# Routing ahead of a mixture of experts: places of two row blocks at once, the last block's expert input on VectorE, gathered rows unfilled, and the fixed experts' first products ahead of the one-hots

## The chip, the cores and the metric

The kernel runs on one core of a Trainium2 chip. The metric is device time in microseconds of one execution; the figure of a kernel is the median of several. The profile is of one execution, whose time is given beside its span.

## The reference

One layer of a hybrid diffusion backbone over 1024 latent tokens of width 1024: a token mixer (a bidirectional state-space branch and a pooling branch, merged by gates), a projection and a first layer norm, then a hierarchical mixture of experts and a second layer norm. The change touches the seam between the mixer and the experts, so this is the part to see:

```python
lg = hf @ w_rg + b_rg                       # 4 groups; the best one is taken
le = (hf @ w_re + b_re)[best group]         # 8 experts in it
top_v, top_i = lax.top_k(le, 2)
w = p_grp * softmax(top_v)
...                                         # every token goes to 2 of 32 experts
y[e] = (silu(x_e @ w_eg[e]) * (x_e @ w_eu[e])) @ w_ed[e]     # 1024 -> 512 -> 1024
out = sum over the two experts of w * y
```

All is f32. Each expert has 6 MiB of weights.

## The kernel before

The kernel is written with a tile framework that orders the instructions of each engine by itself: it models when each could start and lets those that come earlier in the program go first. `tc.issue_after(x)` queues an instruction behind x on its own engine, `tc.high_priority` lets one go ahead of its place in the text. Each engine, SyncE's and POOL's queues too, then runs in the order so fixed.

**The output projection and the choice (loop of lines 1137 to 1179).** The 1024 tokens are 8 row blocks of 128. For block t, `wout` multiplies by the output matrix and adds the residual in r; `turn` transposes r; eight matmuls give 36 router logits (line 1158); `stats` gives mean and 1/deviation (ag, rs); the logits come out on line 1164 (lgt). `choose(t)` (lines 989 to 1023) is a chain of some 17 small VectorE instructions: best group, best expert, second expert, as one-hots o12 and their sum A (line 1020), and running counts bsum. Then r is normalized on ScalarE (line 1166), the expert input hx = r G2 + B2 is made (lines 1172, 1173) and written to h2_d by POOL's queue (line 1174), and r, scaled by the first norm's weights (lines 1177, 1178), goes to r0_d (line 1179). For blocks 0 to 6 hx is made on VectorE and r on POOL; for block 7 the other way round.

**The places.** `place(t)` (lines 1025 to 1051) counts with two matmuls how many tokens ahead of each one chose the same expert, keeps what falls to the three fixed experts (29 to 31, 32 rows each), and adds with a one-hot product to `pidf`, a column of row numbers of the fixed experts' 96 rows. Places are taken with a lag of five blocks: 0, 1, 2 at blocks 5, 6, 7, and 3 to 7 after block 7. The other 29 experts get row blocks by rank of their counts: lines 1267 to 1305 work out rank and capacity on 32 partitions, lines 1306 to 1319 spread that to the tokens, lines 1328 to 1338 form one-hots (ohl, ohh) of all 2048 choices and 16 products that give `pid`, the row numbers of 50 row blocks, and lines 1250 to 1259 turn these into gather and scatter indices xidx and yidx. `tab` (line 1349) holds the experts by rank; SyncE reads it to know which weights to load.

**The experts.** `block` gathers 128 rows of h2_d by index (line 1239, an indirect DMA on POOL's queue), transposes them (line 1389), multiplies by gate and up weights, and by the down weights, scales and scatters. Indices out of range are skipped by the gather, so the first use of each of four buffers xe is preceded by a fill with zeros on POOL (line 1237). The first block is that of the three fixed experts: exact f32 products (line 1406), 32 rows of each, 16 steps for gate and up and 8 for down, in each step two passes over the three experts. Then the dynamic experts follow in the order "DEQEESPESPSPSPSPSPSS" of capacities 256 (D, two blocks), 192 (E), 128 (S), 64 in pairs (P) and 32 in fours (Q), and at the end a loop over experts that overflow.

**Weights.** `load_w` fills slots of one megabyte, 16 in all (`NSA` + `NSB`), in turn. The fixed experts take 24 tiles of 768 KB (three transfers each), so tiles 16 to 23 go into slots 0 to 7 once the first products have read these. Tiles 14 and 15 are issued by POOL behind the first gather (lines 1263 to 1265). All other weights go through SyncE's queue in program order (line 1222).

**PSUM.** `st` and `tr` have one bank each, `mm` four, `py` two. `pos` (counts of all tokens) holds `tr` until line 1316, the ranks hold `st` until line 1312, and `block` transposes through `st` and `tr`.

Of the kernel before, what the change touches and what calls it, by code (L numbers as in the profile page):

```python
# [11 lines left out]
F32 = mybir.dt.float32  # L12
# [8 lines left out]
P = 128  # L21
# [82 lines left out]
LAG = 5  # L104
# [37 lines left out]
def _emit(tc, nc, es, ins, out, dbg, stop):  # L142
# [810 lines left out]
    gp = rg.enter_context(pool("gp", side="right"))  # L953
    r0g = row(gp, ins["ln"][0], "r0g")
    r0b = row(gp, ins["ln"][1], "r0b")
    lgt = gp.tile([P, NT, 36], F32, name="lgt")
    G2 = row(gp, mod_d[0, 2 * D:3 * D], "G2")
    B2 = row(gp, mod_d[0, D:2 * D], "B2")
# [21 lines left out]
    ohhf = gp.tile([P, NT, 2, 4], F32R, name="ohhf")  # L980
# [8 lines left out]
    def choose(t):  # L989
# [28 lines left out]
        A = gp.tile([P, NE], F32, name="A", bufs=LAG + 1)  # L1018
# [5 lines left out]

    def place(t, A):
        def tl(shape, name):
            return gp.tile([P] + shape, F32, name=name, bufs=2)

        T.matmul(pos[:, t], cst[:, C_SPRE], A, start=True, stop=False)
        T.matmul(pos[:, t], ones, bsum[:, t], start=False, stop=True)  # L1030


        pf = pos[:, t, NE - NF:]
        okf = tl([NF], "okf")
        V.tensor_scalar(okf, pf, float(FIX_CAP), None, op0=OP.is_lt)
        pb = tl([NF], "pb")
        V.tensor_tensor(pb, pf, ct[:, 341:341 + NF], op=OP.add)
        of = tl([2, NF], "of")
        V.tensor_tensor(of, o12[:, :, t, NE - NF:], b1_(okf, 2), op=OP.mult)
        lp = tl([2, 2, NF], "lp")  # L1040
        V.tensor_tensor(lp[:, 0], of, b1_(pb, 2), op=OP.mult)
        V.tensor_tensor(lp[:, 1], of, b2(aid.rearrange("p (k t) -> p k t", k=2)[:, :, t], NF), op=OP.mult)
        lv = tl([2, 2], "lv")
        V.tensor_reduce(lv, lp, axis=AX.X, op=OP.add)
        lo = lv[:, 0]
        V.tensor_copy(ohhf[:, t, :, 0], lv[:, 1])
        ohlf = gp.tile([P, 2, P], F32R, name="ohlf", bufs=1)
        last = V.tensor_tensor(ohlf, b1_(iop, 2), b2(lo, P), op=OP.is_equal)
        for k in range(2):
            T.matmul(pidf, ohlf[:, k], ohhf[:, t, k], start=(t + k == 0), stop=(t == NT - 1 and k == 1))  # L1050
        return last

    def weights():
        S.activation(ge, ge, AF.Exp)
        pg = kept.tile([P, NT], F32, name="pg")
        V.tensor_reduce(pg, ge, axis=AX.X, op=OP.add)
        V.reciprocal(pg, pg)
        V.tensor_sub(v12[:, 1], v12[:, 1], v12[:, 0])
# [4 lines left out]
        V.tensor_tensor(wk[:, 1], wk[:, 0], v12[:, 1], op=OP.mult)  # L1063

    with pool("o_sb") as op_:
# [10 lines left out]
        bT2 = gp.tile([P, 4, P], F32, name="bT2")  # L1076
# [60 lines left out]
        for t in range(NT):  # L1137
# [106 lines left out]


    with pool("gq", side="right") as gq:
# [3 lines left out]
        def rows_of(pid, n, name, x, y=None):  # L1250

            fi = tl([n], name + "f")
            V.tensor_scalar(fi, pid, 0.0, 8192.0, op0=OP.is_equal, op1=OP.mult)
            V.tensor_tensor(fi, fi, pid, op=OP.add)
            gi = tl([n], name + "g")
            V.tensor_scalar(gi, fi, float(L + 1), -float(L), op0=OP.is_ge, op1=OP.mult)
            V.scalar_tensor_tensor(x, gi, -1.0, fi, op0=OP.add, op1=OP.add)
            if y is not None:
                V.tensor_scalar(y, fi, -1.0, None, op0=OP.add)

        rows_of(pidf[:, 0:1], 1, "fx", xfix)
        gathered.append(gather(xfix))
# [4 lines left out]
        e32 = slice(0, NE)  # L1267
        fixed, ecol = ct[e32, 337:338], ct[e32, 340:341]
        pc = bank("st")
        cr = pc[:, 0:NE]  # L1270
        cc = pc[e32, NE:NE + 1]
        T.matmul(cr, ones, bsum[:, NT], start=True, stop=True)
        T.matmul(cc, bsum[:, NT], ones[:, 0:1], start=True, stop=True)
        kr = tl([NE], "kr", NE)
        kc = tl([1], "kc", NE)
        V.scalar_tensor_tensor(kr, cr[e32], 32.0, ct[e32, 40:72], op0=OP.mult, op1=OP.add)
        V.scalar_tensor_tensor(kc, cc, 32.0, ct[e32, 336:337], op0=OP.mult, op1=OP.add)
        V.tensor_scalar(kr, kr, kc, None, op0=OP.is_gt)
        rk = tl([1], "rk", NE)
        V.tensor_reduce(rk, kr, axis=AX.X, op=OP.add)  # L1280
        V.scalar_tensor_tensor(rk, fixed, 64.0, rk, op0=OP.mult, op1=OP.add)

        ns_ = len(STEPS)
        cb2 = tl([2, ns_], "cb2", NE)
        V.tensor_scalar(cb2[:, 0], ct[e32, 144:144 + ns_], rk, None, op0=OP.is_gt)
        V.tensor_scalar(cb2[:, 1], ct[e32, 144:144 + ns_], rk, None, op0=OP.min)
        V.tensor_tensor(cb2, cb2, ct[e32, 152:152 + 2 * ns_].rearrange("p (a n) -> p a n", a=2), op=OP.mult)
        cols = tl([3], "cols", NE)
        V.tensor_reduce(cols[:, 0:2], cb2, axis=AX.X, op=OP.add)
        V.tensor_tensor(cols[:, 0:2], cols[:, 0:2], ct[e32, 338:340], op=OP.add)  # L1290
        cap = cols[:, 0:1]

        rem = tl([1], "rem", NE)
        V.tensor_tensor(rem, cc, cap, op=OP.subtract)
        nbx = tl([8], "nbx", NE)
        V.tensor_scalar(nbx, ct[e32, 72:80], rem, None, op0=OP.is_lt)
        nb = tl([1], "nb", NE)
        V.tensor_reduce(nb, nbx, axis=AX.X, op=OP.add)
        po = pc[e32, 64:65]
        T.matmul(po, cst[e32, C_SPRE, 0:NE], nb, start=True, stop=True)  # L1300
        ovs = tl([1], "ovs", NE)
        V.tensor_copy(ovs, po)
# [67 lines left out]

    scat = []

    def block(idx, w, ne, W=P):

# [264 lines left out]
```

## Time and profile before

| | |
|---|---|
| three runs | 2198.86, 2200.76, 2203.87 us; median 2200.76 |
| profiled execution | 2201.33 us, span 2199.5 us |
| busy share of the span | PE 92%, PE weight load 69%, VectorE 61%, ScalarE 41%, POOL 26% |
| mean granted TensorE clock | 0.968 of full speed |
| DMA moved | 441.90 MB, 201 GB/s over the span |

How to read it: busy shares are means over stages with different limits. The first row block's hx is made at 1453 us, the choice and the places run until about 1565, the routing until about 1585, the experts until about 2149, the second norm to the end. A time on the profile counts from the span's start. The granted clock is 1.0 at 2.4 GHz and 0.5 at 1.2 GHz.

### The profile page before, as it was taken

What the parts mean: (1) busy time and instruction counts of PE and PEld (TensorE: products, weight loads), DVE (VectorE), ACT (ScalarE), POOL (GpSimd) and SP (SyncE); (2) the same over time, 40 slices, a digit from 0 to 9 for tenths busy, and PEclk for the clock granted to TensorE, in tenths of its full rate; (3) what the DMA queues carried; (4) which work ended last, traced back from release to release, by engine and by line L of the source; (5) the groups of instructions that cost most, each with busy time, mean ns of one, the idle gap of its engine ahead of it and who ended that gap; (6) DMA issues with size and microseconds to landing.
All of it is one profiled execution on the core that took longest, in us unless ns stands there. A gap on an engine that the chain in (4) does not pass through costs nothing. (4 is left out here: it accounts for less than half of the span.)

```text
span 2199.5 us, 28490 instructions
## 1 busy us (share of the span) xinstructions
PE 2013.6 (92%) x10086; PEld 1524.3 (69%) x10086; DVE 1348.0 (61%) x1913; ACT 895.4 (41%) x1589; POOL 575.7 (26%) x547
## 2 busy tenths in 40 slices
PE   7998999999999999999989999989699899999984
PEld 4787788778777878788768877778455476554451
DVE  4644476677558676867646675587744485543376
ACT  4422254454444564545432232121143364543362
POOL 3243123233224333424200112243411021201003
PEclk8999999999999999999999999999699999999997
DMA  7132233333332333433367675535599999999965
GB/s 296 58 96 87 91 96 106 106 96 96 120 116 91 114 101 93 144 95 108 115 233 245 209 255 166 199 115 191 196 396 341 391 402 389 370 413 411 407 247 234
DMA packets 171899, 441.90 MB, mean 201 GB/s; under 512 B 19997, under 2 KB 54045, under 8 KB 160745
## 3 DMA queue, kind: packets, MB, share of 16 engines
q1 hardware_dynamic: 154282, 399.67, 51.5%
q0 software_dynamic: 9984, 26.75, 3.2%
q10 hardware_dynamic: 7488, 13.63, 1.7%
q8 instruction: 80, 1.31, 0.2%
q14 instruction: 65, 0.53, 0.1%
HBM read 403.01 MB, written 46.28 MB: 204 GB/s over the span
## 5 line engine op out<-in xcount | busy, mean ns | idle before, releaser
L186 PE MATMUL mm<-hh,whi 128*128 128x512 f32 x1024 | 414.8, 405 | 0.0
L188 PE MATMUL mm<-hh,wlo 128*128 128x512 f32 x1024 | 401.5, 392 | 4.2 <-DVE wlo L183 4.2
L187 PE MATMUL mm<-hl,whi 128*128 128x512 f32 x1024 | 400.8, 391 | 0.0
L188 PEld LDWEIGHTS mm<-hh,wlo 128*128 128x128 f32 x1024 | 192.9, 188 | 46.1 <-DVE wlo L183 4.6
L701 ACT ACTIVATE rb<-rb,tmx 128x128 f32<-128x128 f32 x512 | 163.0, 390 | 146.3 <-POOL rb L694 145.0
L186 PEld LDWEIGHTS mm<-hh,whi 128*128 128x128 f32 x1024 | 193.3, 189 | 38.4 <-issue 2.6
L187 PEld LDWEIGHTS mm<-hl,whi 128*128 128x128 f32 x1024 | 193.4, 189 | 35.7 <-issue 0.2
L1367 ACT ACTIVATE sh<-wb 128x512 fp32r<-128x512 f32 x280 | 169.7, 628 | 96.8 <-DMA wb<-in_w_e_dram 24.3
L1368 DVE TENSOR_TENSOR sl<-wb,sh 128x512 fp32r<-128x512 f32 x280 | 180.6, 686 | 39.1 <-ACT sh L1367 33.8
L183 DVE TENSOR_TENSOR wlo<-wraw,whi 128x1024 fp32r<-128x1024 f32 x65 | 82.7, 1272 | 186.1 <-ACT whi L182 186.0
L673 POOL TENSOR_TENSOR st<-st,gst 128x256 f32<-128x256 f32 x112 | 135.6, 1211 | 201.3 <-ACT st L658 120.0
L186 PE MATMUL mm<-zh,bhi 128*128 128x512 f32 x384 | 153.7, 400 | 8.5 <-ACT bhi L182 8.5
L188 PE MATMUL mm<-zh,blo 128*128 128x512 f32 x384 | 153.0, 398 | 1.1 <-DVE blo L183 1.1
L187 PE MATMUL mm<-zl,bhi 128*128 128x512 f32 x384 | 152.0, 396 | 0.3 <-DVE zl L183 0.3
L694 POOL TENSOR_SCALAR_AFFINE_SELECT rb<-rb 128x512 f32<-128x512 f32 x128 | 102.3, 805 | 173.0 <-DMA rb<-sr_d 168.7
L1239 POOL DMA_INDIRECT xe<-h_d,xidx x25 | 27.3, 1091 | 333.7 <-PE tr L1389 304.5
L1406 PE MATMUL mm<-wb,xh 128*64 128x512 f32 (+1 forms) x516 | 108.3, 599 | 0.3 <-ACT xh L1395 0.3
L182 ACT ACTIVATE bhi<-braw 128x1024 fp32r<-128x1024 f32 x48 | 50.8, 1059 | 140.5 <-PE mm L187 123.0
L518 DVE SCALAR_TENSOR_TENSOR xT<-craw,sm,xT 128x1284 f32<-128x1284 f32 x64 | 100.9, 1576 | 2.9 <-ACT xT L516 2.7
L182 ACT ACTIVATE whi<-wraw 128x1024 fp32r<-128x1024 f32 x65 | 68.3, 1050 | 76.5 <-PE mm L187 36.4
L187 PE MATMUL mm<-sl,xh 128*128 128x512 f32 x224 | 88.7, 396 | 5.2 <-DVE sl L1368 5.2
L186 PEld LDWEIGHTS mm<-zh,bhi 128*128 128x128 f32 x384 | 73.2, 191 | 26.0 <-ACT bhi L182 8.9
(471 smaller groups left out, 4094.0 us busy)
## 6 DMA issues: line engine op xcount, KB each, us to landing
wb<-in_w_e_dram SPq DMA_DIRECT2D x70, 1024.0 KB
wb<-in_w_e_dram SPq DMA_DIRECT2D x120, 512.0 KB
wb<-in_w_e_dram SPq DMA_DIRECT2D x142, 256.0 KB
wraw<-in_w_blk_dram SPq DMA_DIRECT2D x64, 512.0 KB
rb<-sr_d SPq DMA_DIRECT2D x128, 256.0 KB
F<-sr_d SPq DMA_DIRECT2D x64, 256.0 KB
wmr<-in_w_ada_dram SPq DMA_DIRECT2D x64, 256.0 KB
braw<-in_wa_blk_dram SPq DMA_DIRECT2D x32, 512.0 KB
```

Source lines behind the costliest of these rows:

```text
L182: S.activation(hi, src, AF.Copy)
L183: V.tensor_sub(lo, src, hi.bitcast(F32))
L186: T.matmul(ps, lh, rh, start=start, stop=False, **kw)
L187: T.matmul(ps, lh, rl, start=False, stop=False, **kw)
L188: return T.matmul(ps, ll, rh, start=False, stop=stop, **kw)
L518: V.scalar_tensor_tensor(o, raw[:, j:j + n], smc(SM_CW + b * KCONV + j), o, op0=OP.mult, op1=OP.add)
L673: G.tensor_tensor(nv, sv, gv[:, s, :, 2 * un:2 * un + 2].unsqueeze(3).to_broadcast([P, 2, 2, 64]), op=OP.mult)
L694: G.affine_select(rv, rv, pattern=[[0, 2], [0, 2], [sg, P]], base=0, channel_multiplier=-sg, compare_op=OP.is_ge, fill=NEG_BIG)
L701: S.activation(e, e, AF.Exp, bias=tmx[:, 0, 2 * n + ih, hd:hd + 1])
L1367: S.activation(hi, w, AF.Copy)
L1368: V.tensor_tensor(lo, w, hi.bitcast(F32), op=OP.subtract)
L1406: T.matmul(pss[0][i * W:(i + 1) * W], ls[0][0][:, k, i * W:(i + 1) * W], wt[:, i], start=(k == 0), stop=(k == nk - 1))
```

## The change

- `place(t0, t1)` takes the places of several blocks with one set of VectorE instructions, twice as wide for two. The schedule is `PLACE_AT`: blocks 0 and 1 at block 5, 2 and 3 at 6, 4 at 7, and after block 7 first 5 and 6, then 7.
- The last block's hx is made on VectorE, at high priority, in two instructions straight from r, mean and deviation, in place of POOL's two products of the normalized r.
- The working out of ranks, capacities and `tab` moves into `ranks()`, directly behind the last places; xfix is made first in it, in three instructions in place of four. The last block's r products on VectorE are queued behind tab, not behind the last place.
- No fill of xe: xfix and the indices of the three row blocks that first use the other buffers are held at zero from below, so that their gathers read rows within range throughout.
- The fixed experts' gathered rows are transposed and multiplied (gate and up) inside the routing, ahead of the text of the one-hots; their transposes go through `mm`. The product that spreads the ranks' table (rows) is queued on PE behind the fourth step of these products.
- The one-hots ohl have two buffers in place of three; the weights of the two choices are worked out behind the last index.
- Allocations move: G2, B2 and lgt come first in their pool, ohlf shares the space of bT2, and the tiles of `ranks` are in a pool of their own.

```diff
-LAG = 5
+PLACE_AT = {5: (0, 2), 6: (2, 4), 7: (4, 5), 8: (5, 7)}
...
-    def place(t, A):
+    def place(t0, t1):
+        n = t1 - t0
...
+        for t in range(t0, t1):
+            T.matmul(pos[:, t], cst[:, C_SPRE], As[t], start=True, stop=False)
+            T.matmul(pos[:, t], ones, bsum[:, t], start=False, stop=True)
...
+        ohlf = gp.tile([P, 2 * n, P], F32R, name="ohlf", tag="bT2", bufs=1)
+        V.tensor_tensor(ohlf, b1_(iop, 2 * n), b2(lv[:, 0], P), op=OP.is_equal)
...
+    def ranks():
...
+        V.tensor_scalar(gi, pidf[:, 0:1], float(L + 1), -float(L), op0=OP.is_ge, op1=OP.mult)
+        V.tensor_tensor(gi, gi, pidf[:, 0:1], op=OP.add)
+        V.tensor_scalar(xfix, gi, -1.0, 0.0, op0=OP.add, op1=OP.max)
...
+        last = V.tensor_copy(tab, pt)
+        return pc, cols, last
...
-                if t >= LAG and n == 0:
-                    place(t - LAG, As[t - LAG])
+                if n == 0 and t in PLACE_AT:
+                    place(*PLACE_AT[t])
...
             As.append(choose(t))
+            hx = op_.tile([P, D], F32, name="hx", bufs=2)
+            if t == NT - 1:
+                with tc.high_priority(offset=HP):
+                    V.scalar_tensor_tensor(hx, r, ag[:, 0:1], G2, op0=OP.subtract, op1=OP.mult)
+                    V.scalar_tensor_tensor(hx, hx, rs, B2, op0=OP.mult, op1=OP.add)
             S.activation(r, r, AF.Identity, scale=rs, bias=nm)
+            if t < NT - 1:
+                V.tensor_tensor(hx, r, G2, op=OP.mult)
+                V.tensor_tensor(hx, hx, B2, op=OP.add)
+            G.dma_start(h2_d[t * P:(t + 1) * P], hx)
             if t == NT - 1:
-                for u in range(NT - LAG, NT):
-                    fence = place(u, As[u])
-            hx = op_.tile([P, D], F32, name="hx", bufs=2)
-            E = G if t == NT - 1 else V
-            E.tensor_tensor(hx, r, G2, op=OP.mult)
-            E.tensor_tensor(hx, hx, B2, op=OP.add)
-            G.dma_start(h2_d[t * P:(t + 1) * P], hx)
+                place(*PLACE_AT[NT])
+                place(PLACE_AT[NT][1], NT)
+                pc, cols, tabbed = ranks()
             E = V if t == NT - 1 else G
-            with tc.issue_after(fence.ins) if t == NT - 1 else ExitStack():
+            with tc.issue_after(tabbed.ins) if t == NT - 1 else ExitStack():
                 E.tensor_tensor(r, r, r0g, op=OP.mult)
...
-        if nblk[0] < NXE:
-            with tc.issue_after(loads[1].ins) if nblk[0] > 1 else ExitStack():
-                G.memset(xe, 0.0)
...
+        xh = gq.tile([P, KD, P], F32, name="xh")
+        for kk in range(2):
+            pt = quad("mm")
+            for i in range(4):
+                T.transpose(pt[:, i], xe[:, (4 * kk + i) * P:(4 * kk + i + 1) * P], ident)
+            S.activation(xh[:, 4 * kk:4 * kk + 4], pt, AF.Copy)
+        begun = []
+        for m in range(2):
+            ps = bank("mm")
+            exact_product(ps, xh, fixed_w, m * KD, KD, NF, FIX_CAP)
+            begun.append([ps])
...
-        T.matmul(rows, ones[e32], dg, start=True, stop=True)
+        with tc.issue_after(marks[0].ins):
+            T.matmul(rows, ones[e32], dg, start=True, stop=True)
...
-                ohl = gq.tile([P, 4, P], F32R, name="ohl", bufs=3)
+                ohl = gq.tile([P, 4, P], F32R, name="ohl", bufs=2)
...
+        gf = tl([NXE - 1], "glf")
+        V.tensor_tensor(gf, gi[:, 1:NXE], pid[:, 1:NXE], op=OP.add)
+        V.tensor_scalar(xidx[:, 1:NXE], gf, -1.0, 0.0, op0=OP.add, op1=OP.max)
+        placed = V.tensor_scalar(yidx, fi, -1.0, None, op0=OP.add)
...
-    weights()
-    block([(xfix, yidx[:, 0:1], False)], fixed_w, len(FIXED), FIX_CAP)
+    weights(placed)
+    block([(xfix, yidx[:, 0:1], False)], fixed_w, len(FIXED), FIX_CAP, begun)
```

## Rows read from the trace of the kernel before

**Rows 1.** Table of windows: start and end us, length, then busy us of PE, PE weight load, VectorE, ScalarE, POOL (instructions), granted clock, DMA share, GB/s.
```profile
1620.00:1640.00 20.00, 19.31 (x88) 15.48 (x86) 11.25 (x17) 10.46 (x18) 0.02 (x1) 1.00 1.01 418
1680.00:1700.00 20.00, 19.57 (x146) 8.12 (x148) 4.67 (x8) 2.60 (x5) 3.25 (x3) 1.00 0.98 337
1700.00:1720.00 20.00, 15.53 (x72) 4.38 (x66) 2.83 (x5) 1.96 (x4) 2.05 (x2) 0.93 0.99 341
1720.00:1740.00 20.00, 16.63 (x56) 8.74 (x54) 7.26 (x11) 6.50 (x11) 1.01 (x1) 0.90 1.01 399
2080.00:2100.00 20.00, 18.46 (x82) 6.00 (x80) 2.00 (x3) 3.64 (x7) 0.00 (x0) 1.00 1.02 422
```
**Rows 2.** Timeline of SyncE's DMA queue: start us, us, then what was issued.
```profile
1544.79 6.87 SPq L1222 DMA_DIRECT2D wb<-in_w_e_dram  x12
1585.14 3.18 SPq L1222 DMA_DIRECT2D wa<-in_w_e_dram  x6
```
**Rows 3.** Waits of SyncE's DMA queue, issues from 1585 to 1612 us: us in total, times, longest.
```profile
SPq L1222 <- PE mm L1406: 34.5, 5, 33.2
```
**Rows 4.** Table of windows, columns as in rows 1, of the routing.
```profile
1560.00:1565.00 5.00, 3.22 (x14) 2.97 (x14) 4.42 (x28) 0.21 (x1) 0.00 (x0) 0.50 0.07 28
...
1580.00:1585.00 5.00, 5.00 (x26) 3.54 (x29) 2.96 (x11) 1.28 (x1) 0.08 (x1) 0.50 0.00 0
1585.00:1590.00 5.00, 5.00 (x30) 1.19 (x27) 0.00 (x0) 0.00 (x0) 4.53 (x5) 0.74 0.70 218
```
**Rows 5.** Timeline of ScalarE: start us, us, the second copy of the fixed experts' transposed rows.
```profile
1576.63 0.60 ACT L1395 ACTIVATE xh<-tr 128x512 f32<-128x512 f32 x1 [0.71 <-PE tr L1389]
```
**Rows 6.** Timeline of PE: start us, us, line, operation, out<-in, count, idle time before and what ended it.
```profile
1563.90 0.59 PE L1050 MATMUL mm<-ohhf,ohlf 128*128 128x4 f32 x2 [0.52 <-DVE ohlf L1048]
...
1574.15 1.08 PE L1389 MATMUL st<-cst,xe 128*128 128x128 f32 x4 [0.85 <-DVE sl__12342 L1313]
...
1579.13 1.05 PE L1338 MATMUL py<-ohh,ohl 128*128 128x50 f32 x4 [2.54 <-DVE ohh L1333]
...
1583.13 3.64 PE L1406 MATMUL mm<-wa,xh 128*32 128x512 f32 x12
...
1614.79 0.50 PE L186 MATMUL mm<-sh,xh 128*128 128x512 f32 x1
```
**Rows 7.** Timeline of POOL, columns as in rows 6.
```profile
1547.03 2.35 POOL L1178 TENSOR_TENSOR r<-r,r0b 128x1024 f32<-128x1024 f32 x1
...
1555.11 2.38 POOL L1173 TENSOR_TENSOR hx<-hx,B 128x1024 f32<-128x1024 f32 x1
...
1567.07 1.86 POOL L1237 MEMSET xe<- 128x1024 f32 x2
1569.83 1.08 POOL L1239 DMA_INDIRECT xe<-h_d,xfix  x1 [0.90 <-POOL xe L1237]
```
**Rows 8.** The gathers (line 1239) by stretch: those issued from 1550 to 1575 us, and from 1586 to 1595; us from issue to landing.
```profile
DMA to landing us min/median/max: 4.2/4.2/4.2
...
L1239 POOL DMA_INDIRECT xe<-h_d,xidx x3: 990/990/1028, 1588.0 to 1590.6; - x3
DMA to landing us min/median/max: 8.7/9.3/9.6
```
**Rows 9.** Timeline of VectorE, columns as in rows 6.
```profile
1551.70 0.26 DVE L1164 SCALAR_TENSOR_TENSOR lgt<-st,brs,lb 128x36 f32<-128x36 f32 x1
...
1552.92 2.14 DVE L1008 TENSOR_SCALAR msk<-rct,gi 128x4 f32<-128x4 f32 x1
...
1555.20 2.31 DVE L1041 TENSOR_TENSOR lp<-of,pb 128x6 f32<-128x6 f32 x1
...
1560.91 0.18 DVE L1020 TENSOR_TENSOR A<-o 128x32 f32<-128x32 f32 x1
...
1563.77 1.22 DVE L1177 TENSOR_TENSOR r<-r,r0g 128x1024 f32<-128x1024 f32 x1
...
1567.04 1.93 DVE L1257 SCALAR_TENSOR_TENSOR xfix<-fxg,fxf 128x1 int32<-128x1 f32 x1
...
1573.34 0.26 DVE L1312 COPY rw<-st 128x96 f32<-128x96 f32 x1 [0.83 <-PE st L1309]
...
1581.16 0.69 DVE L1336 TENSOR_TENSOR ohl<-rct,sf 128x512 fp32r<-128x512 f32 x1
...
1583.95 0.21 DVE L1257 SCALAR_TENSOR_TENSOR xidx<-blg,blf 128x50 int32<-128x50 f32 x1
```
**Rows 10.** The chain that ended last: start us, us; a scalar_tensor_tensor over 128x1024.
```profile
2155.91 1.30 DVE wb L1529
```
**Rows 11.** The write of block 6's hx (line 1174), issued at 1549.3 us: us from issue to landing.
```profile
DMA to landing us min/median/max: 9.3/9.3/9.3
```
**Rows 12.** Timeline of PE's weight loads: each row is one pass over the three fixed experts, the time to the next row is that of a pass.
```profile
1585.70 0.19 PEld L1406 LDWEIGHTS mm<-wb,xh 128*32 128x32 f32 x3 [0.66 <-issue]
1586.55 0.19 PEld L1406 LDWEIGHTS mm<-wb,xh 128*32 128x32 f32 x3 [0.66 <-issue]
...
1588.34 0.12 PEld L1406 LDWEIGHTS mm<-wb,xh 128*32 128x32 f32 x3 [0.31 <-issue]
1588.77 0.12 PEld L1406 LDWEIGHTS mm<-wb,xh 128*32 128x32 f32 x3 [0.31 <-issue]
```
**Rows 13.** The page's DMA queues: packets, MB, share of 16 engines' span.
```profile
q0 software_dynamic: 9984, 26.75, 3.2%
```

More of the change, by code (lines that the diff above doesn't have):

```diff
@@ L1023, in choose @@
         return A
-    def place(t, A):
+    def place(t0, t1):
+        n = t1 - t0
         def tl(shape, name):
[L1027 to L1034, printed above, removed]
-        V.tensor_scalar(okf, pf, float(FIX_CAP), None, op0=OP.is_lt)
[L1036 to L1051, printed above, removed]
@@ new lines, in place, with weights @@
+        V.tensor_copy(ohhf[:, :, t0:t1, 0], lv[:, 1].rearrange("p (k t) -> p k t", k=2))
+        ohlf = gp.tile([P, 2 * n, P], F32R, name="ohlf", tag="bT2", bufs=1)
+        V.tensor_tensor(ohlf, b1_(iop, 2 * n), b2(lv[:, 0], P), op=OP.is_equal)
+        for t in range(t0, t1):
+            for k in range(2):
+                T.matmul(pidf, ohlf[:, k * n + t - t0], ohhf[:, k, t], start=(t + k == 0),
+                         stop=(t == NT - 1 and k == 1))
+    e32 = slice(0, NE)
+    def weights(last):
@@ L1054, in weights @@
         S.activation(ge, ge, AF.Exp)
         pg = kept.tile([P, NT], F32, name="pg")
-        V.tensor_reduce(pg, ge, axis=AX.X, op=OP.add)
-        V.reciprocal(pg, pg)
-        V.tensor_sub(v12[:, 1], v12[:, 1], v12[:, 0])
+        with tc.issue_after(last.ins):
+            V.tensor_reduce(pg, ge, axis=AX.X, op=OP.add)
+            V.reciprocal(pg, pg)
+            V.tensor_sub(v12[:, 1], v12[:, 1], v12[:, 0])
         S.activation(v12[:, 1], v12[:, 1], AF.Exp)
@@ L1243, in gather, with exact_product @@
         return xe
+    def exact_product(ps, xh, w, s0, nk, ne, W):
+        tiles, kc = w
+        for k in range(nk):
+            wt = tiles[(s0 + k) // kc][:, :, (s0 + k) % kc]
+            for i in range(ne):
+                last = T.matmul(ps[i * W:(i + 1) * W], xh[:, k, i * W:(i + 1) * W], wt[:, i], start=(k == 0),
+                                stop=(k == nk - 1))
+            if s0 + k == 3:
+                marks.append(last)
+    marks = []
     with pool("gq", side="right") as gq:
@@ L1248, in tl @@
             return gq.tile([np_] + shape, F32, name=name)
[L1250 to L1262, printed above, removed]
+        xe = gather(xfix)
         for w, src in late:
@@ L1265, in _emit @@
                 G.dma_start(w, src)
[L1267 to L1286, printed above, removed]
@@ L1371, in _emit, with block @@
     scat = []
-    def block(idx, w, ne, W=P):
+    def block(idx, w, ne, W=P, begun=None):
         exact = ne > 1
@@ L1380, in block @@
         xs = []
-        for xi, yi, half in idx:
+        for xi, yi, half in idx if begun is None else ():
             xe = gathered.pop(0) if gathered else gather(xi)
@@ L1401, in product @@
             tiles, kc = w
-            for k in range(nk):
-                wt = tiles[(s0 + k) // kc][:, :, (s0 + k) % kc]
-                if exact:
-                    for i in range(ne):
-                        T.matmul(pss[0][i * W:(i + 1) * W], ls[0][0][:, k, i * W:(i + 1) * W],
-                                 wt[:, i], start=(k == 0), stop=(k == nk - 1))
-                else:
-                    hi, lo = split_w(wt[:, 0], k)
+            if exact:
+                exact_product(pss[0], ls[0][0], w, s0, nk, ne, W)
+            else:
+                for k in range(nk):
+                    hi, lo = split_w(tiles[(s0 + k) // kc][:, 0, (s0 + k) % kc], k)
                     for ps, (lh, ll), (_, _, half) in zip(pss, ls, idx):
@@ L1421, in folded @@
             return dst
-        pgu = []
-        for m in range(2):
+        pgu = begun or []
+        for m in range(0 if begun else 2):
             pss = [bank("mm") for _ in idx]
```

113 lines of the change are left out of this document (75 added, 38 removed).

## The prediction

> **What bounds the kernel now.** I read the expert stage first, since all the edits sit just ahead of it. In the table of windows from 1620 us on [rows 1] the DMA share is 0.98 to 1.02 in the windows shown, at 340 to 420 GB/s, while PE is full up to 1700 us (19.3 and 19.6 of 20 us) and idles between 1700 and 1740 (15.5 and 16.6 of 20). So the stage has two nearly equal bounds, the expert weights' transfer and PE, and where PE got ahead it waited for weights. Both start from the same event. SyncE issues twelve weight transfers at 1544.8 us and then nothing until 1585.14 [rows 2]; the wait, 33.2 us long, ends on a matmul of line 1406 [rows 3]. The 24 tiles of the fixed experts don't fit the 16 slots: tiles 16 to 23, and all later weights behind them in the same queue, wait until the fixed experts' first products have freed slots 0, 1, and so on. That product starts at 1583.13, the queue moves 2.0 us later. The DMA engines idle meanwhile (0.00 of their time from 1580 to 1585) and PE stands at half clock, 0.50 [rows 4]. What ends 1583.13 is therefore the question.
>
> Backwards from there: the gathered rows lay transposed in xh at 1577.23 [rows 5], but PE's order has the one-hot products of line 1338 first, from 1579.13 [rows 6]; 5.9 us. The gather was issued at 1569.83 and took 4.2 us to land [rows 7, 8]. Its index xfix ended at 1568.97 [rows 9], behind two 128x1024 instructions on r (1.22 us each) and stretched to 1.93 us beside POOL's fill of two xe tiles [rows 7, 9]. Before that lies the choice of block 7: its logits at 1551.70, its A at 1560.91 [rows 9]; in between two small VectorE instructions took 2.14 and 2.31 us, where their like take 0.2, in the very time of POOL's two hx products (2.38 us each) [rows 7, 9].
>
> **The change, term by term.** Moment A is the end of block 7's A, 1561.09 before.
>
> hx of block 7 goes from POOL to VectorE, as two scalar_tensor_tensor at high priority. Removed: the two stalls, 2.14 + 2.31 less 0.4 = 4.1 us. Added: two such instructions over 128x1024, 1.2 to 1.3 us each (the nearest row is 1.30 [rows 10]), ahead of the logits since they have priority: 2.5 us. Bounds: 0, should they fall behind the choice, to 2.6. hx would be ready at about 1553.1 instead of 1557.5, and its write issued then. In a loaded queue such a write took 9.3 us [rows 11], so it has landed by 1562.4 at worst, 0.6 us ahead of xfix below: no new wait, with little margin.
>
> The two instructions have two SBUF inputs each. POOL's products on block 6 end at 1549.4 [rows 7], 1.0 us ahead of them. The Trainium skill's GPSIMD Engine Reference, Key points, says that GpSimd shares its SBUF interfaces with VectorE and contends with VectorE instructions that have two SBUF inputs or run in a 2-port mode. By that rule this edit loses, if POOL slips by over a microsecond, what it takes away: one hold of some 2.4 us, and a start 10.5 us earlier in place of the 12.9 below. The trace agrees that VectorE was held while POOL multiplied.
>
> Placing. Blocks go two at a time at blocks 5 and 6, one at 7, and 5, 6 and then 7 after the last. Eight VectorE instructions of about 0.16 us and one one-hot per placing stay, twice as wide. Before, four placings (3 to 6) were woven into the choice of block 7; now two, 5 and 6 at once, are certain to be. Between nothing and 1.6 us (four ohlf of 0.42) saved; I take 0.7. So A comes 4.1 - 2.5 + 0.7 = 2.3 us earlier, at 1558.8.
>
> From A to the first product it took 22.0 us. The new length: placing block 7 is unchanged (A to the end of its pidf product at 1564.49, 3.4 us) [rows 6]. xfix then took 4.5 us, and now has three instructions of 0.16 us, with the r products queued behind tab and no fill to hold them; with the rank instructions woven in, 0.8. The gather follows at once (0.9 us of fill removed): 4.2 us to land [rows 8], 4.3 with the wait. Transposes of two quads and two copies took 3.1 us with a wait for a PSUM bank in them [rows 5, 6]; from the mm banks I take 2.9. Then the products, with no one-hots ahead: 3.4 + 0.8 + 4.3 + 2.9 = 11.4 us. First product at 1570.2, 12.9 us earlier: 2.3 + 10.6.
>
> For the gather, the Trainium skill's DMA: Bandwidth & Descriptors, on the anatomy of a GpSimd DMA, fits 2.0 us plus bytes at 436 GB/s; for 512 KB that is an estimate of 3.2 us, and the sum would be 13.9. The row shows 4.2, and the row decides.
>
> Does a stream that starts 12.9 us earlier stay earlier? The first tiles are there: DMA has nearly stopped by 1560. Tiles 14 and 15 are issued by POOL behind the gather, 3.3 us, and are needed only 14 steps later. PE is cold: one pass over the three experts takes 0.85 us at half clock, 0.43 at full [rows 12], two passes a step. A step frees 768 KB, so even at half clock slots come free at 460 GB/s, more than the queue has carried; the clock costs the stream nothing. Before, about six of the 32 passes ran at half clock, behind 4 us of one-hots [rows 4, 6, 12]; now only 2.3 us of transposes come ahead, so I take ten, between six and all 32: 32 x 0.43 + 10 x 0.42 = 18 us, and the products end at 1588.
>
> The one-hots are now what is late next. Their rows product waits for the fourth step, 1577.0 (no wait on the chip, a place in PE's order); from rw to the last ohl VectorE took 8.5 us [rows 9], so 1586; PE takes them behind the products, 2 to 4 us; xidx at about 1591 against 1584.1. The gathers for the first dynamic expert then fall into a full queue: 8.7 to 9.6 us [rows 8], landed by 1600.5, first product at 1603 against 1614.79 [rows 6], still 11.8 us earlier. Two buffers of ohl instead of three make the last two wait for PE, about 1 us, inside that. tab comes some 16 us earlier, which nothing uses: its first reader sits in SyncE's queue behind the 24 tiles. The weight exponentials now run after the places, with up to two table loads of 1.3 us on ScalarE; the landing of tile 23, some 22 us after the stream's start (1594), hides them.
>
> No fill: out-of-range rows of the next three gathers are now read. All POOL-queue transfers moved 26.75 MB [rows 13]. The 8 hx and 8 r writes and 6 tiles account for 9.96; the other 16.8 are 52 gathers and scatters of at most 0.52 MB, so on average 39% of each is skipped. Full, three gathers cost at most 3.9 us of the stream at 400 GB/s, at least nothing; at 39% they would cost 1.5, and since the first row block of the largest expert is probably full I take 1.0.
>
> Sum: 12.9 - 1.0 = 11.9 us off the profiled execution's 2201.3 (span 2199.5 and 1.8 around it), which lies 0.6 above the median of the runs: 2188.8 us.
>
> **Rivals.**
> (a) POOL takes the last r write ahead of the gather, as the program's text has it. Then the gather waits for tab (about 1566) and two r products, to 1569: 6 us of the gain are lost, 2195. For it: before, that write did stand ahead (the fill came only after it, at 1567.07 [rows 7]). Against it: r now becomes ready long after xfix, and the order on every engine here mixes later lines into earlier ones.
> (b) The weights start early but PE doesn't follow: one-hots behind the down products, and the clock down until then. The first dynamic product comes where it did; the stream runs ahead in its 16 slots, and the gain is what PE idled between 1700 and 1740, 7.8 us [rows 1], less 1.0: 2194.
> (c) Slower: the same, worse. Half clock for all 32 passes ends the products at 1570.2 + 27.4 = 1597.6; the down products at 1.71 us a step, behind 2 us of activation, end at 1613; one-hots 4 us, xidx 1, gather 9.5, transposes 3: first dynamic product at 1630, 15 us later than now. As PE idled 7.8 us later on, it decides from about 1623 on; the end would come 7 us later, 2208. Against it: before, the clock was back at full after six passes [rows 12].
> (d) The change doesn't do what it says: the order that results keeps one-hots ahead of the products and hx late. Of the 12.9 only xfix without r products and fill is left, 3.7 + 0.9, less 1.0 of gathers and 2.5 of hx on VectorE: 2200.
>
> **Chances.** Forecast 0.67; (a) 0.12; (b) 0.10; (d) 0.06; (c) 0.05. A measurement of this kernel tells 0.2%, 4.4 us, from nothing. Faster by more: forecast, (a) and (b), all at least 5.5 us, 0.89; within: (d), 0.06; slower: (c), 0.05. The forecast's own range, 2184 to 2193, comes from the bounds: 2.5 us for hx, 0.9 for placings, 1.0 for the gather, 2.9 for the full rows. The range for 8 in 10 takes in (a) and (b): 2184 to 2196.
>
> **What would show it.** Right: SyncE's long wait ends at about 1572, on a product of the fixed experts; hx of block 7 on VectorE near 1551 to 1553 and no small VectorE instruction of two microseconds after 1550; xfix near 1563 and the gather within a microsecond of it; the expert windows as before, all some 12 us earlier, with the DMA share at 1.0. Wrong: the gather issued after an r write (a); the first dynamic product near 1614 (b) or later (c), with fewer PE idle microseconds around 1700; or one-hots ahead of the products (d).

## The result, and the profile after

The change made the kernel slower: 2223.7 us median against 2202.3, ratio 1.0103 with a 95% interval of 1.0083 to 1.0124. Forecast was 2188.8 with 0.05 for slower. The profiled execution has a span of 2220.0 us, 20.5 above that of the kernel before.

SyncE's DMA queue shows the first of two causes. To read it, one more row of the kernel before is needed: the weight transfers of the fixed tiles 2 to 13, of which [rows 2] has the last twelve (columns: start us, us, what).

```profile
1502.70 48.96 SPq L1222 DMA_DIRECT2D wb<-in_w_e_dram  x36
```

After, the same queue, and under it its longest wait (us in total, times, longest), which answer to [rows 2] and [rows 3]:

```profile
1503.89 0.33 SPq L1175 DMA_DIRECT2D r<-in_x_dram  x1
1579.17 25.67 SPq L1300 DMA_DIRECT2D wb<-in_w_e_dram  x36
1605.23 3.67 SPq L1300 DMA_DIRECT2D wa<-in_w_e_dram  x6
```
```profile
SPq L1513 <- DVE tab L1135: 66.7, 1, 66.7
```

The 36 transfers that lay beside the projection before now start at 1579.17, 76 us later, and tile 16 (the wa row) follows at 1605.23 instead of 1585.14. The wait is on tab at line 1513, the `value_load` of the dynamic experts' numbers. The reads of tab that SyncE made between the r transfer and these 36 (count, then ns min/median/max, then first and last start us):

```profile
L1513 SPq TENSOR_LOAD <-tab x13: 263/266/532, 1571.0 to 1578.5; - x13
```

Thirteen reads of tab stand ahead of the 36 transfers, in one queue with them. The change writes the making of tab ahead of the weights in the program, and the framework, which lets what comes earlier go first, took the reads along; before, the first read came at 1604.98, behind all 24 tiles. In the table of windows (columns as in [rows 1]) the DMA engines stand still from 1565 to 1570 with these weights still to come, where [rows 4] had them already landed, and are full at 1610:

```profile
1565.00:1570.00 5.00, 1.24 (x7) 0.92 (x7) 3.74 (x31) 0.00 (x0) 0.00 (x0) 0.50 0.00 2
1610.00:1620.00 10.00, 3.99 (x16) 1.48 (x19) 0.00 (x0) 0.60 (x1) 1.74 (x2) 0.66 1.04 395
```

The timelines of VectorE, POOL and PE answer to [rows 9, 7, 6] (start us, us, line, operation, idle time before and what ended it):

```profile
1548.60 2.35 DVE L1013 TENSOR_TENSOR lem<-lgt,msk 128x32 f32<-128x32 f32 x1
...
1551.21 2.16 DVE L999 SCALAR_TENSOR_TENSOR e<-lem,v,rct 128x32 f32<-128x32 f32 x1
1553.29 0.67 DVE L1196 SCALAR_TENSOR_TENSOR r<-r,mm 128x512 f32<-128x512 f32 x1
...
1554.98 1.28 DVE L1242 SCALAR_TENSOR_TENSOR hx<-r,bag,G 128x1024 f32<-128x1024 f32 x1
1556.56 1.28 DVE L1243 SCALAR_TENSOR_TENSOR hx<-hx,brs,B 128x1024 f32<-128x1024 f32 x1
...
1558.48 0.25 DVE L1237 SCALAR_TENSOR_TENSOR lgt<-st,brs,lb 128x36 f32<-128x36 f32 x1
...
1563.46 0.19 DVE L1023 TENSOR_TENSOR A<-o 128x32 f32<-128x32 f32 x1
...
1567.58 0.13 DVE L1087 TENSOR_SCALAR xfix<-fxg 128x1 int32<-128x1 f32 x1
...
1570.73 0.21 DVE L1135 CAST tab<-py 1x65 int32<-1x65 f32 x1 [0.54 <-PE py L1134]
...
1595.23 0.26 DVE L1361 COPY rw<-st 128x96 f32<-128x96 f32 x1 [21.74 <-PE st L1358]
...
1606.13 0.20 DVE L1394 SCALAR_TENSOR_TENSOR xidx<-blg,blf 128x50 int32<-128x50 f32 x1
```
```profile
1573.63 0.53 POOL L1257 DMA_DIRECT2D r_d<-r  x1 [14.97 <-DVE dg L1355]
1574.62 1.09 POOL L1314 DMA_INDIRECT xe<-h_d,xfix  x1 [0.46 <-issue]
1607.08 1.05 POOL L1314 DMA_INDIRECT xe<-h_d,xidx  x1 [28.08 <-DVE v L1069]
```
```profile
1580.00 1.97 PE L1347 MATMUL mm<-cst,xe 128*128 128x128 f32 x8 [9.31 <-DMA xe<-h_d,xfix]
1581.90 3.63 PE L1326 MATMUL mm<-wa,xh 128*32 128x512 f32 x12
1586.53 8.29 PE L1326 MATMUL mm<-wb,xh 128*32 128x512 f32 x24 [0.99 <-DMA wb<-in_w_e_dram]
1594.74 0.46 PE L1358 MATMUL st<-dg,cst 32*128 32x96 f32 x2
...
1616.01 1.11 PE L1436 MATMUL st<-cst,xe 128*128 128x128 f32 x4 [7.70 <-DMA xe<-h_d,xidx]
1617.05 5.03 PE L1326 MATMUL mm<-wb,xh 128*32 128x512 f32 x20
...
1635.73 0.50 PE L187 MATMUL mm<-sh,xh 128*128 128x512 f32 x1
```

Read them down: the row numbers xfix are there at 1567.7, but the gather goes at 1574.62, behind the r write (rival (a)); the fixed products begin 1.2 us earlier than before, then wait 1.0 us for weights; the one-hots' start, rw, comes at 1595.23 instead of 1573.34 and xidx at 1606.13 instead of 1583.95; the first dynamic product comes at 1635.73, 20.9 us later than in [rows 6]. The span grew by 20.5. After that product the expert stage is the old one, moved by 20 us ([rows 1]; PE 19.31 of 20 at 1640, and its idle window now at 1720):

```profile
1640.00:1660.00 20.00, 19.31 (x87) 15.70 (x86) 10.82 (x17) 10.56 (x17) 1.03 (x1) 1.00 1.02 422
...
1720.00:1740.00 20.00, 15.15 (x72) 4.38 (x70) 3.52 (x6) 1.96 (x4) 2.05 (x2) 1.00 1.00 348
```

### The profile page after: what moved, and what is told of

Its sections match the earlier page's. It is cut to its first block, busy times and chain, and to the rows that moved or that the text cites. A ratio compares the mean times of both kernels' runs of the same rounds, so it can differ in the third digit from the quotient of the medians.

```text
span 2220.0 us, 28457 instructions
## 1 busy us (share of the span) xinstructions
PE 2023.3 (91%) x10086; PEld 1525.5 (69%) x10086; DVE 1345.8 (61%) x1891; ACT 896.0 (40%) x1589; POOL 571.5 (26%) x541
## 3 DMA queue, kind: packets, MB, share of 16 engines
q0 software_dynamic: 9984, 27.20, 3.2%
## 5 line engine op out<-in xcount | busy, mean ns | idle before, releaser
L1326 PE MATMUL mm<-wb,xh 128*64 128x512 f32 (+1 forms) x516 | 119.8, 606 | 1.2 <-DMA wb<-in_w_e_dram 1.0
L519 DVE SCALAR_TENSOR_TENSOR xT<-craw,sm,xT 128x1284 f32<-128x1284 f32 x64 | 100.2, 1565 | 3.0 <-ACT xT L517 2.9
L187 PEld LDWEIGHTS mm<-zh,bhi 128*128 128x128 f32 x384 | 73.2, 191 | 26.6 <-ACT bhi L183 9.0
```

Source lines behind the costliest of these rows:

```text
L187: T.matmul(ps, lh, rh, start=start, stop=False, **kw)
L519: V.scalar_tensor_tensor(o, raw[:, j:j + n], smc(SM_CW + b * KCONV + j), o, op0=OP.mult, op1=OP.add)
L1326: last = T.matmul(ps[i * W:(i + 1) * W], xh[:, k, i * W:(i + 1) * W], wt[:, i], start=(k == 0), stop=(k == nk - 1))
```

## The experiments

"D" below is the first dynamic block; tile 16 is where the stream of the weights behind the first 16 tiles starts. Ratios are to the kernel before, run on the same chip; "best" stands for e8 and what is built on it. Times of single profiles shift as a whole by several us (block 0's logits came between 1442.7 and 1453.4), so distances are counted from the last residual product on r (block 7's second half; 1547.14 before, 1553.29 after). A row of the table is of one profile, a ratio of several executions.

| kernel | reads of tab | one-hots | tile 16 | D's first product | ratio, 95% |
|---|---|---|---|---|---|
| before | behind the tiles | first | +38.0 | +67.7 | 1 |
| the change | ahead | behind products | +51.9 | +82.4 | 1.0103 (1.0083 to 1.0124) |
| e1 | behind | behind products | +31.0 | +84.3 | 1.0078 (1.0060 to 1.0096) |
| e9 | ahead | first | +56.7 | +83.0 | 1.0085 (1.0063 to 1.0106) |
| e4 | behind | first | +31.0 | +73.2 | 1.0000 (0.9984 to 1.0016) |
| e7 | behind | first | +28.0 | +69.4 | 0.9981 (0.9966 to 0.9997) |
| e8 | behind | first | +28.0 | +58.8 | 0.9971 (0.9957 to 0.9985) |
| e13 | behind | behind products | +27.6 | +78.9 | 1.0034 (1.0017 to 1.0050) |

**e1, the reads behind the tiles.** The changed kernel with one order edit:

```diff
+    fixed_last = qlast[0]            # the last transfer of the fixed tiles
...
-        evs = [nc.sync.value_load(tab[...]) for i in range(ne)]
+        with tc.issue_after(fixed_last.ins):
+            evs = [nc.sync.value_load(tab[...]) for i in range(ne)]
```

> The changed kernel, but SyncE's reads of tab are queued behind the fixed experts' 24 tiles. Theory 1 (the reads of tab, moved ahead of these tiles in SyncE's queue, held 36 weight transfers from about 1503 to 1579 us): the transfers run from 1503 to 1552 as in the kernel before, the first fixed product comes near 1581, tile 16 is issued near 1583 in place of 1605, and the time falls by some 22 us to about 2202 (2197 to 2206). Theory 2 (the loss is in the routing itself: the choice of block 7 is later, the gather stands behind the last r write, the one-hots behind the products): 2215 or more, since none of that is touched. Theory 3 (the projection stage got longer, 4 to 6 us at the last block): 2218 or more.

Measured: 2216.0 us, not the 2197 to 2206 of theory 1 but in the range of theory 2. The 36 transfers are back at 1498.59 and tile 16 at +31.0, 7 us sooner than in the kernel before, yet most of the loss stayed. PE's timeline shows a second cause:

```profile
1610.99 1.11 PE L1438 MATMUL st<-cst,xe 128*128 128x128 f32 x4 [9.77 <-DMA xe<-h_d,xidx]
1612.03 6.15 PE L1328 MATMUL mm<-wb,xh 128*32 128x512 f32 x20
...
1631.83 0.49 PE L187 MATMUL mm<-sh,xh 128*128 128x512 f32 x1
```

The weights are there, but PE idles 9.77 us for D's rows, with the last 20 fixed products queued behind D's transposes, and all down products come after that.

**e2, e1 and the last r write on ScalarE's queue** (`(S if t == NT - 1 else G).dma_start(r0_d...)`), to free the gather of it.

> As the first of these runs, and the last block's r write is issued from ScalarE's queue in place of POOL's, so that the gather of the fixed experts' rows no longer stands behind it. Theory 1 with the forecast's rival (a): the gather moves from 1574.6 to about 1568, the first product to about 1575, tile 16 to about 1577, and the time to about 2195 (2190 to 2199), 6 to 7 us below the first run. If the start of the weights' stream doesn't set the end: within 2 us of the first run.

Measured: 2211.5 us, ratio 1.0052 (1.0034 to 1.0071). Inconclusive: the gather did come 0.8 us behind xfix instead of 6.9, but the edit made a wait of its own: 29 of SyncE's 36 tile transfers waited for this write to land, so tile 16 came at 1598.59:

```profile
SPq L1300 <- DMA r_d<-r: 69.4, 1, 69.4
```

**e3, the kernel before with the ranks and tab moved ahead, nothing else.**

> The kernel before, with only the ranks, capacities and tab worked out ahead of the end of the projection's pool, as the change has it (ohlf shares the space of bT2 to make room). All else as before: single places, hx on POOL, fills, one-hots ahead of the products. Theory 1: one read of tab now stands ahead of the 36 transfers; they start when tab is there, near 1573, run until about 1599, and the time rises to about 2215 (2210 to 2220). Theories 2 and 3: 2199 to 2204, no change.

Measured: 2219.2 us, ratio 1.0096 (1.0075 to 1.0116), as expected of the reads. One read now stands ahead of the 36 transfers, and that is enough:

```profile
1567.26 34.16 SPq L1280 DMA_DIRECT2D wb<-in_w_e_dram  x36
1601.76 3.79 SPq L1280 DMA_DIRECT2D wa<-in_w_e_dram  x6
```

**e4, e1 with the one-hots first again** (the transposes and gate/up products moved behind yidx in the text, no fence on the rows product):

```diff
-        with tc.issue_after(marks[0].ins):
-            T.matmul(rows, ones[e32], dg, start=True, stop=True)
+        T.matmul(rows, ones[e32], dg, start=True, stop=True)
```

> The changed kernel with the reads of tab queued behind the 24 fixed tiles, as in e1, and in addition with the fixed experts' transposes and gate/up products written behind the one-hots and the rows product without its fence (the products-first part of the change undone; places by pairs, hx on VectorE, no fill and the early ranks kept). Theory A, two separate causes (reads of tab ahead of the 36 transfers on SyncE; one-hots late, so D's gather late with the last 20 fixed products queued behind D's transposes): the rows product comes right after tab, xidx near 1584 instead of 1598, D's gather near 1585 instead of 1598.7, PE's idle time before D's transposes under 3 us instead of 9.8, first dynamic product 1613 to 1618 instead of 1631.8, time 2196 to 2203. Theory B (e1's rest is not the order on PE but the earlier weight transfers colliding with the gathers): within 4 us of e1, 2212 to 2218, first dynamic product still past 1627.

Measured: 2202.7 us, ratio 1.0000. The whole loss is gone, which theory A said. Its times within the execution were too early, also counted from the residual product (this profile's came 8 us late): D's transposes still hold up PE, 8.43 us instead of under 3:

```profile
1604.22 0.45 PE L1437 MATMUL st<-cst,xe 128*128 128x128 f32 x1 [8.43 <-DMA xe<-h_d,xidx]
```

**e9, the fourth of four: one-hots first, reads of tab ahead.**

> The changed kernel with only its products-first part undone (transposes and products of the fixed experts written behind the one-hots, rows product without a fence); the reads of tab stay ahead of the 36 fixed-tile transfers on SyncE. It is the fourth of four: neither mended 1.0103 (the change), reads alone 1.0078 (e1), both 1.0000 (e4). Theory A, two causes each of which delays the first dynamic product by itself: the 36 transfers still start behind tab, near 1578, so the gate/up products wait for weights to about 1600 and the weights of the first dynamic expert come 16 to 20 us late; time 2214 to 2224, ratio 1.006 to 1.010. Rival, the one-hots alone are the cause and the reads cost only the 7.7 us that e1 gave back: ratio 1.002 to 1.004, 2206 to 2210.

Measured: 2219.7 us, as theory A had it. On SyncE's queue it is the change again:

```profile
1579.57 30.46 SPq L1300 DMA_DIRECT2D wb<-in_w_e_dram  x36
1610.42 3.67 SPq L1300 DMA_DIRECT2D wa<-in_w_e_dram  x6
```

So each cause alone costs 0.8 to 0.9% and both 1.0%: they delay the same event, D's first product (+82.4 to +84.3 with either or both), and overlap.

**e5, e1 with D's transposes queued on PE behind the last gate/up product** (`with tc.issue_after(marks[2].ins)` around them, for D alone).

> e1 (reads of tab behind the fixed tiles) with one edit: the transposes of the first dynamic block (D) queued on PE behind the last fixed gate/up product, instead of ahead of the last 20. The one-hots stay late. Theory A: PE's 20 products run while D's gather lands (1599 to 1610), the idle time before D's transposes falls from 9.8 to 2 or 3 us, but the gather still lands at 1609 to 1610 and the down products still stand behind; first dynamic product 1622 to 1628, time 2203 to 2210. Theory B: as e1, 2212 to 2218.

Measured: 2208.6 us, ratio 1.0033 (1.0018 to 1.0048): over half of e1's loss is gone. The time is as theory A had it; D's wait is 4.32 us instead of 9.77, not 2 or 3.

**e7, e4 with the r products queued behind xfix instead of tab; e8, e7 with e5's edit.**

```diff
-        V.tensor_scalar(xfix, gi, -1.0, 0.0, op0=OP.add, op1=OP.max)
+        xf_ = V.tensor_scalar(xfix, gi, -1.0, 0.0, op0=OP.add, op1=OP.max)
...
-        return pc, cols, last
+        return pc, cols, xf_         # what the r products of block 7 are queued behind
```

> e4 with one edit: the two products of r of block 7 on VectorE queued behind the row numbers (xfix) instead of behind tab, so that the r write, which stands ahead of the gather on POOL's queue, is issued earlier. The gather of the fixed rows comes near 1565.5 instead of 1568.9, the first fixed product 3 us earlier; tab and the one-hots come 2.5 us later, and so does D's gather. Theory A: the fixed products wait for D or for weights anyway, so within 3 us of e4, either sign. Rival: the start sets the end, 3 us faster than e4.

> e7 and the edit of e5 together: one-hots first, r products behind xfix, D's transposes behind the last fixed gate/up product. If D's gather (near 1588, landing near 1597) is no longer what PE waits for, first dynamic product 1610 to 1616 and time 2192 to 2200, equal to or below the kernel before; if the transposes of D in the middle of the products cost nothing when the rows are there, the same as e7 within 2 us.

Measured: e7 2197.6 us, ratio 0.9981 (0.9966 to 0.9997); e8 2195.3, 0.9971 (0.9957 to 0.9985). By the medians e7 is 5 us faster than e4, more than theory A allowed, but the intervals overlap. e8 beats the kernel before and the change. It can't be told from e7, though its D comes 10.6 us earlier at the same tile 16: with the stream of weights early, D's first product alone no longer sets the time. A second measurement of e8 agrees:

> e8 once more, beside e9, e10 and e11 on one chip: ratio to the kernel before 0.995 to 0.999; 2193 to 2199.

Measured: 2197.2 us, 0.9978 (0.9965 to 0.9992). PE waits less than 1 us for D, and D's first product comes 3 to 6 us earlier in the execution than in [rows 6], 8 to 9 us earlier counted from the residual product:

```profile
1597.39 0.66 PE L1439 MATMUL st<-cst,xe 128*128 128x128 f32 x4 [0.95 <-DMA xe<-h_d,xidx]
...
1611.62 0.50 PE L187 MATMUL mm<-sh,xh 128*128 128x512 f32 x1
```

**e13, e8 with the products ahead of the one-hots again.** The reads, the r products and D's place on PE are mended here, so it prices the change's main idea by itself.

> e8 with the one part put back that gives the change its name: transposes and gate/up products of the fixed experts written ahead of the one-hots, and the rows product fenced behind the fourth step. Reads of tab stay behind the fixed tiles, r's products behind xfix, D's transposes behind the last gate/up product. If products first is a loss by itself (the one-hots come 12 to 14 us later, so D's gather lands after the products have ended): first dynamic product some 60 us behind xfix instead of 44.5, ratio to the kernel before 1.000 to 1.003, 2202 to 2207, against 0.9971 and 0.9978 of e8. If it only suffered from the order on SyncE and from D's transposes, both mended here: as e8 or better, 0.994 to 0.998.

Measured: 2207.0 us, ratio 1.0034 (1.0017 to 1.0050), against 0.9971 and 0.9978: products first costs 0.6%, as the first expectation had it. D's gather came at 1600.83, its rows at 1613.34, and the first product 18.6 us behind those:

```profile
1613.34 1.12 PE L1440 MATMUL st<-cst,xe 128*128 128x128 f32 x4 [6.57 <-DMA xe<-h_d,xidx]
...
1617.98 3.64 PE L1328 MATMUL py<-wa,ehh 128*32 128x512 f32 x12
...
1631.90 0.50 PE L187 MATMUL mm<-sh,xh 128*128 128x512 f32 x1
```

**e10, e8 with hx of block 7 on GpSimd; e11, e8 with the fills back.**

> e8 with hx of block 7 back on GpSimd behind ScalarE's r, as before the change. lgt of block 7 comes some 3.5 us earlier (the two products on VectorE, 1.28 us each, stand ahead of it in e8), but GpSimd's two products take about 9 us beside the placings and stretch them, hx's write is issued 4 to 6 us later, and the gather waits for its landing. If hx on VectorE gains what the prediction gave it (POOL's stalls 4.1 against 2.5 of its own): 1 to 3 us slower than e8, 2195 to 2199. If lgt sets the start: 1 to 3 us faster.

> e8 with the fills of the gathered rows back on GpSimd (two ahead of the first gather, two behind it). The fills ahead of the gather run while GpSimd waits for r's write, so the gather is later by at most 1 us; the prediction's term was 1.0 us. Time within 2 us of e8, 2194 to 2199; over 3 us would mean that the fills collide with VectorE's chain of one-hots.

Measured: e10 2197.6 us, 0.9987 (0.9969 to 1.0004); e11 2204.2, 1.0011 (0.9998 to 1.0024). The hx move can't be told from nothing. In e10's trace two held instructions (small ones of VectorE that take some 2 us instead of 0.2) are back in block 7's choice, while without hx ahead of them the logits come 0.8 us sooner behind the residual product (4.45 us against 5.20):

```profile
1552.09 2.19 DVE L1024 TENSOR_TENSOR bsum<-bsum,A 128x32 f32<-128x32 f32 x1
...
1554.37 2.29 DVE L999 SCALAR_TENSOR_TENSOR g<-lgt,gmax,rct 128x4 f32<-128x4 f32 x1
```

The fills cost more than the 1 or 2 us expected: 0.3%. The two ahead of the gather take 1.86 us as before. Beside them one small VectorE instruction of the ranks took 2.42 us, and tab came 7.5 us behind xfix instead of 5.1. With them the order on PE comes out otherwise, too: the fixed transposes are split by the one-hots, and the first fixed product comes 17.3 us behind xfix instead of 11.5 to 11.8.

```profile
1566.28 2.42 DVE L1116 TENSOR_SCALAR nbx<-rct,rem 32x8 f32<-32x8 f32 x1
```
```profile
1574.10 1.11 PE L1398 MATMUL mm<-cst,xe 128*128 128x128 f32 x4 [2.03 <-DMA xe<-h_d,xfix]
1577.99 1.02 PE L1381 MATMUL py<-ohh,ohl 128*128 128x50 f32 x4 [2.78 <-DVE ohh L1376]
...
1580.65 1.92 PE L1331 MATMUL mm<-wa,xh 128*32 128x512 f32 x2
```

How the 0.3% divides between the two is not shown: it is read from one trace, and neither was tried alone.

**e14 and e15, e8 with other placings.** One thing was left. From block 0's logits to block 7's last residual product it is 95.5 us before and 95.6 in e3, but 98.5 to 102.6 in the twelve profiles with the new placing. VectorE in the kernel before, at the residual product, to be set beside the first three VectorE rows of after above:

```profile
1544.67 2.33 DVE L996 SCALAR_TENSOR_TENSOR e<-lem,v,rct 128x32 f32<-128x32 f32 x1
...
1547.14 0.68 DVE L1123 SCALAR_TENSOR_TENSOR r<-r,mm 128x512 f32<-128x512 f32 x1
1547.74 1.68 DVE L1014 TENSOR_SCALAR o<-rct,e1i 128x32 f32<-128x32 f32 x1
```

Of the two held instructions of block 6's choice one stands ahead of the residual product before, both after: the placing of block 4 at block 7 puts VectorE behind, so more of block 6's choice falls beside GpSimd's r products.

```diff
-PLACE_AT = {5: (0, 2), 6: (2, 4), 7: (4, 5), 8: (5, 7)}
+PLACE_AT = {5: (0, 1), 6: (1, 2), 7: (2, 3), 8: (3, 4)}   # e14, and 4 to 7 singly
+PLACE_AT = {5: (0, 2), 6: (2, 4), 8: (4, 6)}              # e15
```

> e8 with the placing as before the change: one row block at blocks 5, 6 and 7 (blocks 0, 1, 2) and blocks 3 to 7 singly after the last. Theory C, a third cost of the change that the prediction did not have: the placing of block 4 at block 7, and the pairs ahead of it, put VectorE behind in the projection, so that the residual product of block 7's second half falls behind two VectorE instructions held beside GpSimd's r products (2.35 and 2.16 us) instead of one. From block 0's logits to that product it is 95.5 us in the kernel before (95.6 in e3, which has the old placing) and 98.5 to 102.6 in every kernel with the new one. By C it is 95 to 98 here, and the time 2 to 4 us under e8, ratio 0.9955 to 0.9965, less what five single placings cost after the last block (1 to 2 us). Rival: the 3 to 7 us come from hx or from the order of the later code, then it stays at 98 to 102 and the time is that of e8 or 1 to 2 us above.

> e8 with pairs, but none at block 7: blocks 0 and 1 at block 5, 2 and 3 at 6, and 4 and 5, then 6 and 7 after the last. By theory C the distance from block 0's logits to block 7's second residual product is 95 to 98 us (in e8 101.6 and 98.5), block 7's choice to the row numbers at most 1 us longer than in e8, and the time 2194 or below, ratio 0.995 to 0.9965. Rival as in e14: distance 98 to 102, ratio 0.997 to 0.998.

Measured: e14 2193.6 us, 0.9969 (0.9951 to 0.9987); e15 2191.5, 0.9962 (0.9944 to 0.9979), the fastest here. The distances are 98.8 and 98.1 us, just past the 95 to 98 of theory C and inside its rival's 98 to 102, so the whole distance doesn't decide; its last part does. In e15 one held instruction is left ahead of the residual product, as before the change:

```profile
1538.31 2.33 DVE L999 SCALAR_TENSOR_TENSOR e<-lem,v,rct 128x32 f32<-128x32 f32 x1
...
1540.78 0.68 DVE L1196 SCALAR_TENSOR_TENSOR r<-r,mm 128x512 f32<-128x512 f32 x1
```

From block 5's second residual product to block 7's it is 20.1 us before, 22.4 after, 20.1 in e14 and 20.3 in e15: this 2.4 us is the placing's. The other 1 to 5 us lie further ahead, in stretches with a lower granted clock. One of these returns: from block 7's first residual product to block 5's second, PE does nearly the same work in 8.8 us at full clock before and in e3, in 9.35 at full clock in e5, and in 10.4 to 11.0 at a granted clock of 0.84 in the other thirteen profiles of the changed kernel and its variants. Windows of before, e5 and after, columns as in [rows 1]:

```profile
1518.28:1527.09 8.81, 8.66 (x52) 7.38 (x51) 3.56 (x24) 0.60 (x1) 0.00 (x0) 1.00 0.80 250
1512.14:1521.49 9.35, 9.23 (x58) 8.06 (x57) 3.68 (x18) 0.60 (x1) 0.00 (x0) 1.00 0.83 278
1519.91:1530.85 10.94, 10.82 (x58) 9.20 (x57) 3.66 (x17) 0.60 (x1) 0.00 (x0) 0.84 0.00 0
```

Why the clock fell there stays open. In time neither e14 nor e15 can be told from e8.

## Why the prediction was wrong

1. **The order on SyncE; this step failed first.** "tab comes some 16 us earlier, which nothing uses: its first reader sits in SyncE's queue behind the 24 tiles." It sat there because of where tab was made; moving that moved the reads ahead of 36 transfers (e3: 0.96% by itself). The prediction counted the moved step's instructions on VectorE and PE, and took its readers' place from the trace of before as fixed.

2. **D behind the late one-hots; this failed too, and would have sufficed** (e13, with the reads, the r write and D's place mended, is slower than the kernel before). The sizes up to xidx were right where the weights were there: in e13 rw comes 7.3 us behind the first product (6.8 predicted) and xidx 14.0 behind rw (14). Wrong was "landed by 1600.5, first product at 1603", 2.5 us from rows to product. From D's transposes, which start once the rows are there, it is 18.6 in e13 and 19.7 in the change, and it was 19.1 before already, since D's transposes stand on PE ahead of SwiGLU and all 48 down products: in the trace of before the transposes are at 1595.74 and the product at 1614.79. With 19 us in place of 2.5 the prediction's own landing gives about 1619.5, 4.7 us later than before in place of 11.8 earlier. The landing was mis-sized too: from xidx to the rows it is 13.5 us in e13, 9.5 predicted. Rival (c) came near in its numbers, 1630 and 2208 us; e13, whose profile ran some 6 us late, measured 1631.9 and 2207.0. That is partly luck. (c) had the down products ahead of D, which is right, but put the one-hots behind them and all 32 passes at half clock; in e13 the one-hots lie amid the gate and up products, whose granted clock was 0.76.

3. **The gather behind the r write: rival (a).** It happened. The row numbers came as predicted, xfix ending 4.1 us behind A (3.4 + 0.8). But in the change the gather comes 6.9 us behind xfix, and takes 5.3 us to land, not 4.2 [rows 8]. From the Trainium skill's DMA: Bandwidth & Descriptors (Anatomy of one DMA, SWDGE path) the estimate for the landing is 3.2 us; the measurement decides. With the r products queued behind xfix the gather comes 3.9 us behind xfix in e7 and e8. From A to the first product it took 18.2 us, not 11.4.

4. **hx and the places.** The two held instructions of block 7's choice went, as predicted, and hx's two instructions took 1.28 us each. From the last residual product to A it is 14.0 us before and 10.4 after: 3.6 us gained, 2.3 predicted; with hx back on GpSimd (e10) it is 12.9. Some of this was only moved: block 6's second held instruction lay behind that residual product and now lies ahead of it. Block 7's last residual product came 6.2 us later behind block 0's logits (95.5 against 101.7). Of this 2.4 us are the placing of block 4 at block 7 (e14, e15), which the prediction put at nothing; the rest lies in the stretches of lower clock. The Trainium skill's GPSIMD Engine Reference, Key points, says that GpSimd contends with VectorE instructions that have two SBUF inputs or run in a 2-port mode. In these traces hx's two instructions with two SBUF inputs were not held, starting 1.1 us or more after GpSimd's products had ended; 128x32 ones beside those products, with one or two inputs, took 1.5 to 2.4.

5. **The gathered rows.** All POOL-queue transfers moved 27.20 MB instead of 26.75 [rows 13], 0.45 more: 1.1 us at 400 GB/s against the 1.0 taken. The bytes were sized right; what they cost in time no run shows by itself.

6. **What an earlier start is worth.** In e8, with the reads, the r write and D's place mended and the one-hots first again, the stream's tile 16 comes 10 us earlier behind the residual product and D 8 to 9 us earlier, and e8 and e15 gain 0.2 to 0.4%, 5 to 8 us, of the 11.9 forecast. The stage ahead takes 3 to 6 us of it back. The forecast took an earlier D to be worth its whole lead; between e7 and e8 10.6 us of D were worth at most a few us, too little to be told from nothing.

## What to carry to other kernels

When a step is moved in a program whose engines' orders are made for you, follow the readers of its result too: an early result can pull a blocking read ahead of transfers in the same queue, and one read ahead (e3, 0.96%) costs as much as thirteen (e9, 0.85%). "First product behind the landing" is a distance to be read from the trace, with everything that the engine's order puts between. An order that feeds the second consumer late to start the first one early is priced by the second consumer's whole path.

## What the runs showed of the hardware

- Each of SyncE's reads of tab took 0.63 us on average in the change, 0.26 to 0.53 for the load and the rest for register steps behind it: thirteen filled the time from 1570.94, when tab was written, to 1579.17, and no transfer left that queue meanwhile.
- A write moved to ScalarE's queue held back 29 of SyncE's transfers for 69.4 us (e2); in the trace the write and the first of these signal their landing on the same semaphore.
- VectorE's 128x4 and 128x32 instructions take up to 2.4 us instead of 0.2 beside GpSimd's 128x1024 products in each of these kernels. With hx's two products off GpSimd the two held ones of block 7's choice are gone (e8), and with hx back there they return (e10).
